# A state-space mixer whose norm adds up a group's squares one tile of weights later

## The chip, the core and the metric

The kernel runs as one program on one core of a Trainium2 chip. A core has engines with a queue of instructions each: TensorE (PE in the rows, with PEld for the loading of weights into it), VectorE (DVE), ScalarE (ACT), GpSimd (POOL) and SyncE (SP, which here issues transfers). They run side by side and wait for one another by semaphores. The time is the device time of one launch in microseconds. Three runs of the kernel before took 2009.55, 2011.78 and 2013.37 us; their median, 2011.78 us, is the time that is compared.

## What is computed

The reference is a block of a diffusion generator with two layers over 512 tokens of 1024 channels (256 context tokens, 256 latent tokens). Layer 0 mixes tokens by a state-space scan (SSD), layer 1 by retention, and each ends in a mixture of experts. The change lies in the SSD mixer, in the last step of `ssd_branch`:

```python
y = y_f + rev(y_b) + xs * d_skip.reshape(SSD_GROUPS, SSD_HPG)[..., None]
y = y.reshape(bsz, seqlen, SSD_D_INNER) * jax.nn.silu(proj[..., :SSD_D_INNER])
yg = y.reshape(bsz, seqlen, SSD_GROUPS, SSD_D_INNER // SSD_GROUPS).astype(jnp.float32)
yg = yg * lax.rsqrt(jnp.mean(jnp.square(yg), -1, keepdims=True) + LN_EPS)
return yg.reshape(bsz, seqlen, SSD_D_INNER).astype(dtype) * norm_w, h_f, h_b
```

The 2048 inner channels form four groups of 512. For each token and group the output of the scan is multiplied by a gate, and the result is divided by the root of the mean of its squares over the group. That root's reciprocal is called the factor here: 512 tokens by 4 groups, kept as a 128x4 tile for each group. It is used only when the output projection is evicted, since it can be multiplied in behind that product.

## The kernel before

The class `SSD` runs over a list `tiles` of weight tiles: `dt`, then for each group three `x` tiles (convolution inputs: one channel block each for the scan's B and C, and four for x) and two `z` tiles (the gate), then the output tiles `o`. A weight tile comes in by a transfer into a ring (`ringA`), ScalarE rounds it to a short form (`wh`, line 440) and GpSimd subtracts to get the remainder (`wl`, line 441). A block of 128 channels takes 24 products of 128x512 into the PSUM tile `pin`, eight steps of three products each: lines 719, 720 and 721. For an `x` block ScalarE copies `pin` to `pad` and starts `cacc`, VectorE adds the four other taps of the convolution (line 750), ScalarE takes a tanh (`cth`, line 752) and VectorE finishes `cacc` (line 759). TensorE transposes it (`ptr`, line 733) and ScalarE stores it as `xtok` (line 734). For a `z` block ScalarE takes a tanh (`zth`) and VectorE makes `sz` (line 777).

Beside these tiles runs work of the groups. The dictionary `side` says behind which tile each piece is called, and the table `PACE` gives the place as an offset from the last `x` tile of the group: the scan's start (`do_scan`), its four chunks (`do_chunk`), and the gate (`do_gate`). In the list the last `x` tile of group g is followed by `z` 0 and `z` 1 of g and then by `x` 0, 1 and 2 of group g+1, so offset 4 is the tile `x` 1 of group g+1 and offset 5 its `x` 2, behind which the scan of g+1 also starts. The calls fix what waits for what. The order in which the instructions then stand on each engine is drawn up by the framework's scheduler; scans and chunks are called at a raised priority. An engine takes its instructions strictly in that order.

The gate makes four rounds of transposes (line 1029) and products with `sz` (line 1031) into `yT`. Then ScalarE squares `yT` (line 1035), GpSimd adds the squares in two steps (lines 1036 and 1037), TensorE adds over partitions by four products with a column of ones (`pms`, line 1040), VectorE scales (`ms`, line 1042) and takes a reciprocal square root by small steps on 128x4 (`rsq`: lines 220 to 223, which each read one tile, and three rounds of 228, 229 and 230, which each read two), and copies the factor to `srs` (line 1045). For groups 0 to 2 `yT` is stored to memory by a transfer (`ytd`, line 1048).

The start of a scan makes `xs` on GpSimd (line 946, from `xtok`), the products `pcb` (line 961) and `ph` (line 948) on TensorE, and copies `ph` to the state `h` on VectorE (line 951). `ph` has one PSUM buffer (tag `y`), so the second `ph` waits for the copy of the first. `ptr`, `pms` and `pcb` share a tag of two buffers (`tp`). GpSimd also makes `sk` (line 1000).

Of the kernel before, what the change touches and what calls it, by code (L numbers as in the profile page):

```python
# [11 lines left out]
F32 = mybir.dt.float32  # L12
# [10 lines left out]
P = 128  # L23
# [113 lines left out]
class Ring:  # L137
# [3 lines left out]
    def __init__(self, nc):  # L141
        self.nc, self.src, self.at, self.tiles, self.pending = nc, [], {}, {}, []
        self.pools, self.finished, self.slot = {}, set(), {}
# [66 lines left out]
def col(S, name, a=0, b=None):  # L210
    o, w = CL[name]
    return S.c[:, o + a:o + (w if b is None else b)]


def rsqrt(S, v, n, eps, pool):

    V = S.nc.vector
    t = pool.tile([P, 4, n], F32, name="rsq", tag="rsq%d" % n, bufs=2)
    x, y, h, q = (t[:, j] for j in range(4))
    V.tensor_scalar(x, v, eps, None, op0=OP.add)  # L220
    V.tensor_scalar(q.bitcast(I32), x.bitcast(I32), 1, None, op0=OP.logical_shift_right)
    V.tensor_scalar(y.bitcast(I32), q.bitcast(I32), -1, 0x5F3759DF, op0=OP.mult, op1=OP.add)
    V.tensor_scalar(h, x, -0.5, None, op0=OP.mult)
    for _ in range(3):
        if n == 1:
            V.scalar_tensor_tensor(q, y, h, y, op0=OP.mult, op1=OP.mult)
        else:
            V.tensor_tensor(q, y, y, OP.mult)
            V.tensor_tensor(q, q, h, OP.mult)
        V.scalar_tensor_tensor(y, q, 1.5, y, op0=OP.add, op1=OP.mult)  # L230
    return y
# [328 lines left out]

SSD_MODS = [(0, 1), (0, 2), (1, 0)]

PACE = [(0, 1, 2, 3, 3, 4)] * 3 + [(0, 0, 1, 1, 1, 3)]


PRI = (0, 0)
# [4 lines left out]
class SSD:  # L571
    def __init__(self, S, A):
        self.S, self.A = S, A
        tiles = [("dt",)] + [("x", 0, q) for q in range(3)]
        for g in range(3):
            tiles += [("z", g, u) for u in range(2)] + [("x", g + 1, q) for q in range(3)]
        tiles += [("z", 3, u) for u in range(2)]
        for g in range(4):
            tiles += [("o", g, u) for u in range(2)]

        self.side = side = {t: [] for t in tiles}
        side["x", 0, 1].append(("steps",))
        for g in range(4):
            at = tiles.index(("x", g, 2))
            for it, n in zip([("scan", g)] + [("chunk", g, c) for c in range(4)] + [("gate", g)], PACE[g]):
                side[tiles[at + n]].append(it)
        side["z", 3, 1] += [("early", 0), ("ysplit", 0)]
        side["o", 2, 1].append(("early", 1))
        side["o", 0, 0] += [("close",), ("ysplit", 1)]
        side["o", 1, 0].append(("ysplit", 2))  # L590
        side["o", 2, 0].append(("ysplit", 3))
        mods = deque(("m", l, q, k) for l, q in SSD_MODS for k in range(8))
        for t in tiles[2:26]:
            if mods:
                side[t].append(mods.popleft())
        self.tiles = tiles
# [422 lines left out]
    def do_gate(self, g):  # L1019

        S = self.S
        nc, w1, w2 = S.nc, self.w1, self.w2
        V, AC, T_ = nc.vector, nc.scalar, nc.tensor
        y, sz = self.y, self.sz.pop(g)
        yT = self.yT[g] = self.yp.tile([P, 4, 512], F32, name="yT")
        for c in range(4):
            pt = self.psum([P, 4, 128], "ptr", "tp")
            for j in range(4):
                T_.transpose(pt[:, j, :], y[:, c, j * 128:(j + 1) * 128], col(S, "ident"))
            t = slice(c * 128, (c + 1) * 128)  # L1030
            V.tensor_tensor(yT[:, :, t], pt, sz[:, :, t], OP.mult)

        sq = [w2.tile([P, 2, 512], F32, name="sq", tag="ee") for _ in range(2)]
        for j in range(2):
            AC.activation(sq[j], yT[:, 2 * j:2 * j + 2], AF.Square)
        nc.gpsimd.tensor_tensor(sq[0], sq[0], sq[1], OP.add)
        nc.gpsimd.tensor_tensor(sq[0][:, 0], sq[0][:, 0], sq[0][:, 1], OP.add)
        pm = self.psum([P, 4], "pms", "tp")
        for i in range(4):
            T_.matmul(pm[:, i:i + 1], sq[0][:, 0, i * 128:(i + 1) * 128], S.ones[:, 0:1], start=True, stop=True)  # L1040
        ms = w2.tile([P, 4], F32, name="ms")
        V.tensor_scalar(ms, pm, 1.0 / 512, None, op0=OP.mult)
        rs = rsqrt(S, ms, 4, 16 * EPS, w2)
        self.rs[g] = S.const.tile([P, 4], F32, name="srs", tag="srs%d" % g)
        V.tensor_copy(self.rs[g], rs)
        if g < 3:
            S.ytd[g] = S.dram.tile([P, 2048], F32, name="ytd", tag="ytd%d" % g)
            nc.sync.dma_start(S.ytd[g], yT.rearrange("p a l -> p (a l)"))


    def norm_setup(self, pool):
# [27 lines left out]
    def build(self):  # L1079
        S, A = self.S, self.A  # L1080
        nc = S.nc
        V, AC, G = nc.vector, nc.scalar, nc.gpsimd
        with ExitStack() as es, ExitStack() as es2:
# [39 lines left out]
            bcast(S, A["ssd_d_skip"], self.dsk)  # L1123
            AC.activation(self.nega, self.dtc[:, 1:2], AF.Exp)
            V.tensor_scalar(self.nega, self.nega, -1.0, None, op0=OP.mult)
            self.Btok, self.BT, self.CT, self.sz, self.yT, self.yhl, self.rs = ({} for _ in range(7))
            S.ytd = {}
            tiles = self.tiles
            prep = lambda n: split_tile(S, tiles[n], self.wp)
# [1152 lines left out]
```

## Time and profile before

| What | Value |
|---|---|
| Median of three runs | 2011.78 us |
| The profiled execution | 2005.95 us |
| Its span | 2004.2 us |
| Mean granted TensorE clock | 0.954 of full |
| TensorE busy | 1769.8 us, 88% |
| VectorE busy | 953.0 us, 48% |
| ScalarE busy | 489.4 us, 24% |
| GpSimd busy | 456.8 us, 23% |

The span is the time between the first and the last instruction of the profiled execution; its own time has 1.75 us around it. Busy shares are means over stages with different limits: the SSD mixer lies between about 90 and 600 us of the span, the first mixture of experts follows it. A row of a timeline gives a start, a duration, an engine, a line, an operation with what it writes and reads, and a count; a bracket at its end is the idle time of that engine ahead of it and what ended it. A queue's order does not tell times, and a busy engine may be one that is held.

### The profile page before, as it was taken

What the parts mean: (1) busy time and instruction counts of PE and PEld (TensorE: products, weight loads), DVE (VectorE), ACT (ScalarE), POOL (GpSimd) and SP (SyncE); (2) the same over time, 40 slices, a digit from 0 to 9 for tenths busy, and PEclk for the clock granted to TensorE, in tenths of its full rate; (3) what the DMA queues carried; (4) which work ended last, traced back from release to release, by engine and by line L of the source; (5) the groups of instructions that cost most, each with busy time, mean ns of one, the idle gap of its engine ahead of it and who ended that gap; (6) DMA issues with size and microseconds to landing.
All of it is one profiled execution on the core that took longest, in us unless ns stands there. A gap on an engine that the chain in (4) does not pass through costs nothing. (4 is left out here: it accounts for less than half of the span.)

```text
span 2004.2 us, 23517 instructions
## 1 busy us (share of the span) xinstructions
PE 1769.8 (88%) x9021; PEld 1002.5 (50%) x9021; DVE 953.0 (48%) x1685; ACT 489.4 (24%) x827; POOL 456.8 (23%) x275
## 2 busy tenths in 40 slices
PE   6899999999986999998999789988897998788886
PEld 3665666666764433332332488776873432123221
DVE  3847575765696434433243566474454432103112
ACT  2555454543212100000000233232232100000000
POOL 2343425343345000000000243454551100000000
PEclk8999999999997999999999899999997999989998
DMA  7423323336735999999999744474367999999996
GB/s 284 150 99 116 126 95 136 111 111 220 275 109 223 371 399 399 373 383 401 409 406 368 290 149 146 155 263 145 113 255 294 409 409 409 409 375 407 409 409 242
DMA packets 138022, 543.84 MB, mean 271 GB/s; under 512 B 10320, under 2 KB 10832, under 8 KB 125360
## 3 DMA queue, kind: packets, MB, share of 16 engines
q1 hardware_dynamic: 137328, 541.80, 69.9%
q8 instruction: 73, 1.20, 0.2%
q10 hardware_dynamic: 576, 0.48, 0.1%
q14 instruction: 45, 0.37, 0.0%
HBM read 537.00 MB, written 5.24 MB: 271 GB/s over the span
## 5 line engine op out<-in xcount | busy, mean ns | idle before, releaser
L441 POOL TENSOR_TENSOR wl<-ringA,wh 128x1024 fp32r<-128x1024 f32 x116 | 290.0, 2512 | 812.0 <-ACT wh L440 794.0
L440 ACT ACTIVATE wh<-ringA 128x1024 fp32r<-128x1024 f32 x118 | 124.3, 1058 | 225.5 <-PE pin L720 61.0
L720 PE MATMUL pin<-u,wh 128*128 128x512 f32 x304 | 132.0, 434 | 0.0
L1868 PE MATMUL pd<-ringB,hT 128*32 128x512 f32 (+1 forms) x472 | 123.0, 617 | 6.0 <-ACT hT L1858 4.5
L721 PE MATMUL pin<-u,wl 128*128 128x512 f32 x304 | 127.4, 419 | 0.0
L719 PE MATMUL pin<-u,wh 128*128 128x512 f32 x304 | 126.9, 417 | 0.0
L1879 DVE SCALAR_TENSOR_TENSOR yh<-pd,ws,yh 128x512 fp32r<-128x512 f32 x40 | 30.0, 751 | 198.1 <-ACT yh L1878 196.2
L1839 PE MATMUL pg<-ringE,xT 128*32 128x512 f32 (+1 forms) x312 | 110.4, 609 | 7.7 <-DMA ringE<-in_moe_w_gate_up_dram 7.2
L1839 PE MATMUL pu<-ringE,xT 128*32 128x512 f32 (+1 forms) x312 | 110.6, 609 | 3.6 <-DMA ringE<-in_moe_w_gate_up_dram 3.6
L1844 ACT ACTIVATE th<-pg 128x512 f32<-128x512 f32 x22 | 13.1, 597 | 402.9 <-PE pg L1839 392.8
L1848 DVE SCALAR_TENSOR_TENSOR th<-th,pg 128x512 f32<-128x512 f32 x22 | 15.1, 687 | 200.0 <-ACT th L1844 200.0
L750 DVE SCALAR_TENSOR_TENSOR cacc<-pad,cw,cacc 128x512 f32<-128x512 f32 x96 | 94.3, 986 | 13.6 <-ACT cacc L748 12.7
L2143 POOL TENSOR_TENSOR oacc<-oacc,ringX 128x512 f32<-128x512 f32 x1 | 1.6, 1623 | 432.6 <-ACT oacc L207 432.6
L1201 PE MATMUL pin<-u,wh 128*128 128x256 f32 (+1 forms) x256 | 84.9, 332 | 16.1 <-DVE gT L1253 10.0
L1911 DVE TENSOR_TENSOR tl<-pc,ringB 128x512 f32<-128x512 f32 x124 | 81.1, 685 | 37.1 <-PE pc L1886 35.3
L1839 PE MATMUL pg<-ringB,xT 128*32 128x512 f32 (+1 forms) x268 | 89.2, 613 | 5.9 <-DMA ringB<-in_moe_w_gate_up_dram 5.9
L1839 PE MATMUL pg<-ringA,xT 128*32 128x512 f32 (+1 forms) x244 | 85.7, 617 | 6.7 <-DMA ringA<-in_moe_w_gate_up_dram 6.2
L1778 PEld LDWEIGHTS px<-oh,hhl 128*128 128x128 f32 x576 | 73.3, 193 | 34.7 <-issue 32.2
L1839 PE MATMUL pu<-ringB,xT 128*32 128x512 f32 (+1 forms) x268 | 89.6, 609 | 0.9 <-DMA ringB<-in_moe_w_gate_up_dram 0.8
L1886 PE MATMUL pc<-yh,os 128*128 128x512 f32 x248 | 82.6, 432 | 8.0 <-DVE tl L1911 7.4
L1868 PE MATMUL pd<-ringE,hT 128*32 128x512 f32 (+1 forms) x240 | 77.1, 601 | 10.0 <-DMA ringE<-in_moe_w_down_dram 7.2
L1839 PE MATMUL pu<-ringA,xT 128*32 128x512 f32 (+1 forms) x244 | 83.1, 615 | 1.8 <-DMA ringA<-in_moe_w_gate_up_dram 1.8
(414 smaller groups left out, 3907.5 us busy)
## 6 DMA issues: line engine op xcount, KB each, us to landing
ringE<-in_moe_w_gate_up_dram SPq DMA_DIRECT2D x76, 1024.0 KB, 18.1
ringB<-in_moe_w_gate_up_dram SPq DMA_DIRECT2D x63, 1024.0 KB, 17.3
ringA<-in_moe_w_gate_up_dram SPq DMA_DIRECT2D x55, 1024.0 KB, 17.6
ringB<-in_moe_w_down_dram SPq DMA_DIRECT2D x53, 1024.0 KB, 18.0
ringA<-in_mod_w_dram SPq DMA_DIRECT2D x40, 1024.0 KB, 4.9
ringF<-in_moe_w_gate_up_dram SPq DMA_DIRECT2D x34, 1024.0 KB, 17.7
ringX<-in_moe_w_gate_up_dram SPq DMA_DIRECT2D x28, 1024.0 KB, 18.1
ringE<-in_moe_w_down_dram SPq DMA_DIRECT2D x28, 1024.0 KB, 18.2
```

What stands on the lines that cost most here:

```text
L440: S.split = nc.scalar.activation(hi, w, AF.Copy).ins
L441: (eng or nc.gpsimd).tensor_tensor(lo, w, hi.bitcast(F32), OP.subtract)
L719: S.nc.tensor.matmul(p, h, self.uh(k), start=k == 0, stop=False)
L720: S.nc.tensor.matmul(p, h, self.ul(k), start=False, stop=False)
L721: S.nc.tensor.matmul(p, l, self.uh(k), start=False, stop=k == 7)
L750: nc.vector.scalar_tensor_tensor(acc, pad[:, :, t:t + 256], cw[:, m, t:t + 1], acc, op0=OP.mult, op1=OP.add)
L1201: self.S.nc.tensor.matmul(p, a, self.uh(k)[:, T], start=k == 0, stop=False)
L1778: nc.tensor.matmul(px[:, b, :], self.S.hhl[i][:, m, j * 128:(j + 1) * 128], oh[:, i], start=i == 0 and m == 0, stop=i == nt - 1 and m == 1)
L1839: nc.tensor.matmul(po[o:o + n, :], xT[:, k, a:a + n], w.get(k)[:, u * 512:(u + 1) * 512], start=k == 0, stop=k == 7)
L1868: nc.tensor.matmul(pd[u % n][o:o + m, :], hT[:, j, a:a + m], w.get(8 + j)[:, u * 512:(u + 1) * 512], start=j == 0, stop=j == 3)
L1886: self.S.nc.tensor.matmul(pc, os_[s, i * 128:(i + 1) * 128], ys[q][s, u % n], start=q == 0, stop=q == 1)
L1911: V.tensor_tensor(t, pc, self.gate(i)[:, c], OP.mult)
```

## The change

The part of the gate behind the two additions on GpSimd becomes a function of its own, `do_factor`. `PACE` gets a seventh entry for it: 5 for groups 0 to 2, which is one tile behind the gate, and 3 for group 3, the same tile as the gate. The tile with the added squares is kept in a dictionary between the two calls, and the store of `yT` is called right behind the additions. No instruction is added or removed.

```diff
-PACE = [(0, 1, 2, 3, 3, 4)] * 3 + [(0, 0, 1, 1, 1, 3)]
+PACE = [(0, 1, 2, 3, 3, 4, 5)] * 3 + [(0, 0, 1, 1, 1, 3, 3)]
...
-            for it, n in zip([("scan", g)] + [("chunk", g, c) for c in range(4)] + [("gate", g)], PACE[g]):
+            for it, n in zip([("scan", g)] + [("chunk", g, c) for c in range(4)] + [("gate", g), ("factor", g)], PACE[g]):
...
         nc.gpsimd.tensor_tensor(sq[0], sq[0], sq[1], OP.add)
         nc.gpsimd.tensor_tensor(sq[0][:, 0], sq[0][:, 0], sq[0][:, 1], OP.add)
+        self.sq[g] = sq[0]
+        if g < 3:
+            S.ytd[g] = S.dram.tile([P, 2048], F32, name="ytd", tag="ytd%d" % g)
+            nc.sync.dma_start(S.ytd[g], yT.rearrange("p a l -> p (a l)"))
+
+    def do_factor(self, g):
+
+        S, w2, sq = self.S, self.w2, self.sq.pop(g)
+        V, T_ = S.nc.vector, S.nc.tensor
         pm = self.psum([P, 4], "pms", "tp")
         for i in range(4):
-            T_.matmul(pm[:, i:i + 1], sq[0][:, 0, i * 128:(i + 1) * 128], S.ones[:, 0:1], start=True, stop=True)
+            T_.matmul(pm[:, i:i + 1], sq[:, 0, i * 128:(i + 1) * 128], S.ones[:, 0:1], start=True, stop=True)
         ms = w2.tile([P, 4], F32, name="ms")
         V.tensor_scalar(ms, pm, 1.0 / 512, None, op0=OP.mult)
         rs = rsqrt(S, ms, 4, 16 * EPS, w2)
         self.rs[g] = S.const.tile([P, 4], F32, name="srs", tag="srs%d" % g)
         V.tensor_copy(self.rs[g], rs)
-        if g < 3:
-            S.ytd[g] = S.dram.tile([P, 2048], F32, name="ytd", tag="ytd%d" % g)
-            nc.sync.dma_start(S.ytd[g], yT.rearrange("p a l -> p (a l)"))
```

What stands where then? First TensorE's queue behind the gate of group 0, as the difference between before (-) and now (+); `ptr` here is the transpose of an `x` block of group 1, and the changed kernel's line 1048 is line 1040 of before.

```order
 L719 MATMUL pin<-u,wh 128x512
 L720 MATMUL pin<-u,wh 128x512
-L721 MATMUL pin<-u,wl 128x512
-L719 MATMUL pin<-u,wh 128x512
-L1040 MATMUL pms<-ones,sq 128x1 x4
-L720 MATMUL pin<-u,wh 128x512
-L721 MATMUL pin<-u,wl 128x512
-L719 MATMUL pin<-u,wh 128x512
-L720 MATMUL pin<-u,wh 128x512
 L733 MATMUL ptr<-c,cacc 128x128 x4
```

The first `ptr` now stands six products, and the squares' four, earlier than before. The second `ptr`, which has kept its place among the products, stands 20 of them behind the first, where it was 14.

Next the same queue some rows later, at the start of the scan of group 1; the `L720` of the second row is the fourth product behind the second `ptr`.

```order
 L719 MATMUL pin<-u,wh 128x512
 L720 MATMUL pin<-u,wh 128x512
+L1048 MATMUL pms<-ones,sq 128x1 x4
+L721 MATMUL pin<-u,wl 128x512
+L719 MATMUL pin<-u,wh 128x512
 L961 MATMUL pcb<-CT,BT 128x128 x4
 L948 MATMUL ph<-xs,Btok 128x512
```

The squares' products now stand ahead of `pcb`, with two products between; four products and the second `ph` follow `ph` in both kernels.

Then VectorE's queue at that place, before: the small steps end ahead of `sz` (line 777), and the copy of the first state `h` (line 951) comes right behind it.

```order
L228 TENSOR_TENSOR rsq<-rsq 128x4
L759 SCALAR_TENSOR_TENSOR cacc<-cth,cacc 128x512
L229 TENSOR_TENSOR rsq<-rsq 128x4
L230 SCALAR_TENSOR_TENSOR rsq<-rsq 128x4
L228 TENSOR_TENSOR rsq<-rsq 128x4
L229 TENSOR_TENSOR rsq<-rsq 128x4
L230 SCALAR_TENSOR_TENSOR rsq<-rsq 128x4
L1045 COPY srs<-rsq 128x4
L777 SCALAR_TENSOR_TENSOR sz<-zth,pin 128x512
L951 COPY h_1571<-ph 128x512
```

And now:

```order
L777 SCALAR_TENSOR_TENSOR sz<-zth,pin 128x512
L220 TENSOR_SCALAR rsq<-ms 128x4
L221 TENSOR_SCALAR rsq<-rsq 128x4
L223 TENSOR_SCALAR rsq<-rsq 128x4
L222 TENSOR_SCALAR rsq<-rsq 128x4
L228 TENSOR_TENSOR rsq<-rsq 128x4
L229 TENSOR_TENSOR rsq<-rsq 128x4
L230 SCALAR_TENSOR_TENSOR rsq<-rsq 128x4
L228 TENSOR_TENSOR rsq<-rsq 128x4
L229 TENSOR_TENSOR rsq<-rsq 128x4
L230 SCALAR_TENSOR_TENSOR rsq<-rsq 128x4
L951 COPY h_1571<-ph 128x512
```

Ten of the small steps have come to stand between `sz` and the copy of `h`; ahead of line 759 there are none now. In group 1 all thirteen and the copy to `srs` stand ahead of the copy of `h`, in group 2 six of them and an addition of the scan's (`ee`, line 987). GpSimd's queue has the same order as before in groups 0 and 1: two `xs`, `sk`, and then a `wl` and two `xs` in group 0, the two `xs` and then a `wl` in group 1; in group 2 the `wl` has moved ahead of the third `xs`. The rest of the queues of these groups is the same but for neighbours that change places, save that in group 2 the first `ptr` stands among products of a modulation, ahead of where `pms` was.

## Rows read from the trace of the kernel before

**Rows 1.** Busy time by stretch of 100 us (stretch, its length, busy us and count of PE, PEld, DVE, ACT and POOL, granted clock, DMA share, GB/s): a stretch of the SSD stage, and one of the expert stage behind it.

```profile
200.00:300.00 100.00, 94.21 (x452) 64.89 (x452) 66.79 (x97) 46.31 (x84) 37.79 (x33) 1.00 0.30 110
...
700.00:800.00 100.00, 93.60 (x559) 37.30 (x552) 39.40 (x75) 7.71 (x15) 0.00 (x0) 1.00 1.02 404
```

**Rows 2.** Whom TensorE waited for between 180 and 520 us (total us, times, longest us).

```profile
PE pms L1040 <- POOL sq L1037: 9.7, 4, 3.3
```

**Rows 3.** Timeline around the squares' products of group 0; columns: start in us, duration in us, engine, line, operation, tiles and shapes, count, and in brackets the idle time ahead with what ended it.

```profile
197.04 2.46 DVE L759 SCALAR_TENSOR_TENSOR cacc<-cth,cacc 128x512 f32<-128x512 f32 x1 [1.14 <-ACT cth L752]
...
197.73 0.39 PE L720 MATMUL pin<-u,wh 128*128 128x512 f32 x1
...
199.42 1.75 DVE L750 SCALAR_TENSOR_TENSOR cacc<-pad,cw,cacc 128x512 f32<-128x512 f32 x1
200.58 2.83 POOL L441 TENSOR_TENSOR wl<-ringA,wh 128x1024 fp32r<-128x1024 f32 x1
...
200.67 1.05 PE L1040 MATMUL pms<-ones,sq 128*128 128x1 f32 x8 [2.08 <-POOL sq L1037]
...
201.84 2.12 DVE L750 SCALAR_TENSOR_TENSOR cacc<-pad,cw,cacc 128x512 f32<-128x512 f32 x1
...
204.80 0.74 DVE L750 SCALAR_TENSOR_TENSOR cacc<-pad,cw,cacc 128x512 f32<-128x512 f32 x1
...
205.58 0.63 ACT L752 ACTIVATE cth<-cacc 128x512 f32<-128x512 f32 x1 [1.76 <-DVE cacc L750]
...
206.33 0.68 DVE L759 SCALAR_TENSOR_TENSOR cacc<-cth,cacc 128x512 f32<-128x512 f32 x1
...
207.07 0.66 PE L733 MATMUL ptr<-c,cacc 128*128 128x128 f32 x4 [0.68 <-DVE cacc L759]
```

**Rows 4.** The same timeline, a little later: the start of the scan of group 1.

```profile
207.48 0.48 PE L720 MATMUL pin<-u,wh 128*128 128x512 f32 x1
...
207.80 0.39 PE L721 MATMUL pin<-u,wl 128*128 128x512 f32 x1
...
208.03 0.40 PE L719 MATMUL pin<-u,wh 128*128 128x512 f32 x1
...
208.44 2.04 POOL L946 TENSOR_TENSOR xs<-xtok,tokv 128x512 f32<-128x512 f32 x2 [2.69 <-ACT xtok L734]
208.49 1.08 PE L961 MATMUL pcb<-CT,BT 128*128 128x128 f32 x8
...
209.54 1.12 PE L948 MATMUL ph<-xs,Btok 128*128 128x512 f32 x2
...
210.70 0.69 DVE L951 COPY h<-ph 128x512 f32<-128x512 f32 x1 [1.09 <-PE ph L948]
...
211.51 0.30 PEld L948 LDWEIGHTS ph<-xs,Btok 128*128 128x128 f32 x2 [0.36 <-POOL sk L1000]
```

**Rows 5.** Timeline, the same place of group 1.

```profile
301.15 2.47 DVE L759 SCALAR_TENSOR_TENSOR cacc<-cth,cacc 128x512 f32<-128x512 f32 x1 [1.93 <-ACT cth L752]
...
304.80 1.05 PE L1040 MATMUL pms<-ones,sq 128*128 128x1 f32 x8 [2.09 <-POOL sq L1037]
...
305.97 2.09 DVE L750 SCALAR_TENSOR_TENSOR cacc<-pad,cw,cacc 128x512 f32<-128x512 f32 x1
...
313.36 2.22 DVE L1045 COPY srs<-rsq 128x4 f32<-128x4 f32 x1
...
315.52 2.04 POOL L946 TENSOR_TENSOR xs<-xtok,tokv 128x512 f32<-128x512 f32 x2
...
316.61 1.12 PE L948 MATMUL ph<-xs,Btok 128*128 128x512 f32 x2 [1.82 <-POOL xs L946]
```

**Rows 6.** Timeline, the same place of group 2.

```profile
403.48 0.68 DVE L759 SCALAR_TENSOR_TENSOR cacc<-cth,cacc 128x512 f32<-128x512 f32 x1
...
407.22 0.40 PE L719 MATMUL pin<-u,wh 128*128 128x512 f32 x1
...
409.71 2.35 POOL L441 TENSOR_TENSOR wl<-ringA,wh 128x1024 fp32r<-128x1024 f32 x1
...
409.80 1.05 PE L1040 MATMUL pms<-ones,sq 128*128 128x1 f32 x8 [2.18 <-POOL sq L1037]
```

**Rows 7.** Small steps of a reciprocal square root elsewhere (the norm behind the mixer), in the timelines of POOL (first row) and of DVE (the next two).

```profile
582.23 2.83 POOL L207 TENSOR_TENSOR tok<-oacc,sca 128x1024 f32<-128x1024 f32 x1
...
582.74 0.20 DVE L207 TENSOR_SCALAR rsq<-rsq 128x1 int32<-128x1 int32 x2
582.98 2.10 DVE L207 SCALAR_TENSOR_TENSOR rsq<-rsq 128x1 f32<-128x1 f32 x1
```

**Rows 8.** All instructions on the tiles rsq, one row of them: duration in ns, least, median and most.

```profile
L229 DVE TENSOR_TENSOR rsq<-rsq x12: 155/161/165, 205.9 to 495.6; 128x4 f32<-128x4 f32 x12
```

**Rows 9.** Busy time by stretch of 10 us, columns as in the first group.

```profile
200.00:210.00 10.00, 8.65 (x47) 6.92 (x48) 7.86 (x21) 3.47 (x6) 5.10 (x6) 1.00 0.48 174
300.00:310.00 10.00, 7.91 (x37) 6.03 (x32) 8.18 (x12) 4.12 (x7) 6.90 (x5) 0.83 0.65 220
...
410.00:420.00 10.00, 10.00 (x50) 7.80 (x50) 7.32 (x27) 5.27 (x12) 3.43 (x3) 0.83 0.38 140
490.00:500.00 10.00, 9.52 (x32) 7.95 (x33) 6.47 (x22) 1.75 (x2) 0.61 (x2) 0.66 0.88 325
```

**Rows 10.** The transfers of expert weights into the ring E among the instructions on that tile: issue time in ns, first and last start in us.

```profile
L186 SPq DMA_DIRECT2D ringE<-in_moe_w_gate_up_dram x76: 368/1790/5597, 468.4 to 1944.1; - x76
```

More of the change, by code (lines that the diff above doesn't have):

```diff
@@ L1125, in build @@
             V.tensor_scalar(self.nega, self.nega, -1.0, None, op0=OP.mult)
-            self.Btok, self.BT, self.CT, self.sz, self.yT, self.yhl, self.rs = ({} for _ in range(7))
+            self.Btok, self.BT, self.CT, self.sz, self.yT, self.yhl, self.rs, self.sq = ({} for _ in range(8))
             S.ytd = {}
```

## The prediction

> **What bounds the kernel now.** I read the stretches first, then the waits, then the timelines of the three places. In the SSD stage TensorE is busy 94.21 of 100 us and the transfers 0.30 of it; in the expert stage behind it the transfers are busy throughout, 1.02 [rows 1]. So in the SSD stage time is lost where TensorE stands still. The expert weights do not start early enough to take such a loss back: the first of their transfers is issued at 468.4 us, behind all three places that the change touches [rows 10]. I count a microsecond of TensorE's idle time there as one of the end.
>
> Of those idle times the longest sum in 180 to 520 us is that of the squares' products, which wait for GpSimd's second addition: 9.7 us in four [rows 2]. Three belong to groups 0 to 2: 2.08, 2.09 and 2.18 us [rows 3, 5, 6]. The fourth is group 3's, which the change leaves where it was. Near them are smaller ones: in group 0 one of 0.68 us for the second transpose [rows 3] and one of 0.36 for the second state product `ph` [rows 4], in group 1 one of 1.82 for the first `ph` [rows 5]. That makes 3.12, 3.91 and 2.18 us at the three places.
>
> **What sets VectorE's pace.** The reader should see one thing in [rows 3]: line 759 has an ordinary length of 0.68 us (206.33), but the one at 197.04 took 2.46, and the next two instructions took 1.75 and 2.12 instead of 0.74. Each ended some 0.55 us behind an instruction of GpSimd: for the third this is visible, GpSimd's `wl` ending at 203.41 and VectorE's line 750 at 203.96. So while GpSimd works, VectorE's instructions with two tiles from SBUF get through one for each of GpSimd's. Group 1 shows the same lengths, 2.47 and 2.09 [rows 5]. It also holds the tiny ones: a step of the reciprocal root took 2.10 us beside GpSimd's 2.83 [rows 7], the copy of the 128x4 factor 2.22 [rows 5]; free, such a step takes 0.16 [rows 8] (0.2 with its handover). Steps that read one tile passed, two in 0.20 [rows 7], and so does the copy of `h`, which reads PSUM, 0.69 [rows 4].
>
> A page speaks against that last reading in part. By the Trainium skill, "SBUF — State Buffer", section "Who interferes with whom", steps that multiply by a constant can enter a mode that takes the shared pair of ports too, and would then be held like the others. The row of 0.20 us shows that they weren't; by the page the copy of `h` in group 0 would come some 0.7 us later, an estimate, and the sum would be up to 2 us higher over three groups.
>
> **The change, part by part.** Nothing is added or removed, so the cost is in waits alone. The store of `yT` is called earlier but waited for no small step before; SyncE has nothing behind it that TensorE awaits here: 0.
>
> *The wait for the squares goes.* The additions end at 200.67, and the products that read them now stand behind the second transpose, about 208: saved 2.08, 2.09 and 2.18 us.
>
> *The first transpose waits in its place.* It stands two products before the old place of the squares. TensorE got there at 200.67 - 2.08 = 198.59, less two products of 0.23 (the spacing at 207.80 and 208.03 [rows 4]) = 198.13. It reads line 759's result, which is held until 199.50, and 0.06 us of handover (207.01 to 207.07 in [rows 3]): idle 1.43. Group 1 the same: 301.15 + 2.47 + 0.06 = 303.68, against 304.80 - 2.09 - 0.46 = 302.25: 1.43. In group 2 line 759 ended at 404.16, ahead of the additions [rows 6]: 0.
>
> *The second transpose.* TensorE does four transposes (0.41, from 207.07 to 207.48) and 20 products, the first taking 0.32 to the next, the others 0.23 [rows 4], and a last one of 0.39 to its end: it is there at 199.56 + 0.41 + 0.32 + 18 x 0.23 + 0.39 = 204.82. VectorE's chain is still held until 203.96, as now; then two taps of 0.74, the tanh of 0.63, line 759 of 0.68 [rows 3] and 0.12 of handovers end at 206.87. Idle 2.05. Group 1: VectorE 305.97 + 2.09 + 2.91 = 310.97 [rows 5], TensorE 303.68 + 5.26 = 308.94: 2.05. Group 2: the third tap is held by `wl` until 409.71 + 2.35 + 0.55 = 412.61, then comes an addition of the scan (0.68), one tap, the tanh and line 759: 415.4. TensorE passes the old place at 407.62 (the product of 407.22 ended then [rows 6]) and has 19 products of 0.23 to do, counting four of the decay's like the others: 412.0. Idle 3.4.
>
> *The second `ph`.* Here the small steps stand ahead of the copy of `h`, and GpSimd is at work. Group 0: the squares' products start at 206.87 + 0.41 + 1.01 = 208.3 and take about 0.9, two products 0.55, so `pcb` starts at 209.75. From `pcb` to the place of the second `ph` it was 211.51 - 0.36 - 208.49 = 2.66 us [rows 4]: TensorE arrives at 212.4. VectorE has `ms` at 209.4, `sz`, four steps that pass, and then six that don't. GpSimd starts `xs` 1.37 us behind the transpose (207.07 to 208.44 [rows 3, 4]), so 208.24; the pair takes 2.04, `sk` as much as one of them, 1.02, `wl` 2.35 when itself not delayed [rows 6], the third `xs` 1.02. The first three held steps go out at 211.3, 213.65 and 214.65. The fourth `xs` waits for the second `ph`, so GpSimd rests, and three steps of 0.2 and the copy of 0.69 end at 216.0: idle 3.6. Group 1: `pcb` at 310.97 + 0.41 + 1.01 + 0.9 + 0.55 = 313.8, first `ph` reached at 314.9, but its `xs` still stands behind a `wl` and starts at 315.52 [rows 5]: ready at 316.55, idle 1.65. The second `ph` is reached 1.6 later, at 318.2; nine steps and the copy to `srs` stand ahead of `h`. `wl`, two `xs`, `sk` and the third `xs` let five through by 319.65, the other five take 1.0, the copy 0.69: 321.35, idle 3.15. Group 2: `pms` at 417.1, `pcb` at 418.6, second `ph` reached at 421.2; the addition `ee` and two steps go out behind `sk` (419.9), `wl` (422.3) and the third `xs` (423.3), the copy ends at 424.0: idle 2.8.
>
> *Sum of the idle times.* Group 0: 1.43 + 2.05 + 3.6 = 7.1 against 3.12, +4.0. Group 1: 1.43 + 2.05 + 1.65 + 3.15 = 8.3 against 3.91, +4.4. Group 2: 0 + 3.4 + 2.8 = 6.2 against 2.18, +4.0. Together +12.4.
>
> *The clock.* Behind the gaps of groups 1 and 2 a stretch of 10 us shows a granted clock of 0.83, a part of it at 1.2 instead of 2.4 GHz: 1.7 us lost in each. Behind group 0's gap of 2.08 it stayed at 1.00, behind group 3's of 3.33 it is 0.66: 3.4 lost [rows 9]. So gaps of 2.1 us sometimes bring a fall and one of 3.3 did. Now four gaps are of 2.8 us and more, and I count 1.7 us for each, less the two falls that go: +3.4. The bounds: no more falls than now, 0; or 3.4 for each of the four and 1.7 for the two of 2.05, less 3.4: +13.6.
>
> Total +15.8. The profiled execution of before, 2005.95 us with a span of 2004.2, would become 2021.75; it lies 5.8 below the median of the runs, 2011.78, and to that I add: **2027.6 us**.
>
> **Rivals.** *The wait changes its place and no more.* The first two transposes wait as above, but the small steps slip through beside GpSimd. For it: the steps that read one tile passed [rows 7], and the twelve of one kind (line 229) never took more than 0.165 [rows 8]. Against it: 2.10 and 2.22 us [rows 5, 7]. Then the idle times are 1.43 + 2.05 + 0.4 = 3.9, 1.43 + 2.05 + 1.65 = 5.1 and 3.4: +0.8, +1.2 and +1.2, one fall of the clock fewer, -1.7: +1.5, **2013.3**, with one fall more or less 2011.6 to 2015. That the change does nothing that can be measured would read the same.
>
> *Faster: VectorE's chain arrives first.* If line 759 and the taps were issued ahead of GpSimd's additions, each at its free length, the first `cacc` would be done 1.8 us sooner (0.68 in place of 2.46), the second some 2.4 (0.74 for 1.75 and 2.12), and both transposes would find it. Then idle time of 0.4 and 1.65 is left in groups 0 and 1: -2.7, -2.3, in group 2 -2.2, and the clock gives back 3.4: **2001.2**. It decides where line 759 ends before 198.1. Against it: the change leaves what stands ahead of line 759, and GpSimd's first addition, as they were, and the row that shows 2.46 is of them [rows 3].
>
> **Chances.** The forecast 0.63, the first rival 0.22, the faster one 0.12, others 0.03. A difference under 0.2% (4 us) can't be told from none in a measurement of this kernel. The forecast is slower by more than that even at 2018, where half the idle time and no clock is lost; its own range is 2018 to 2037. The whole range reaches down to the first rival and leaves out the faster one: 2008 to 2036. Faster 0.14, same 0.23, slower 0.63.
>
> **What would show it.** Right: no wait of TensorE for GpSimd's additions in groups 0 to 2, but waits of 1.4 and 2.05 us for `cacc` and of 2.8 to 3.6 for the copy of `h`; steps of the reciprocal root of 1 to 2.4 us ahead of that copy; lower granted clock at 210, 320 and 420 us. Wrong: small steps of 0.16 us beside `sk` and `wl` (the first rival), or line 759 of group 0 at 0.7 us (the second).

## The result and the profile after

Six runs of the changed kernel gave 2018.79 to 2024.35 us with a median of 2022.82; six of the kernel before, in the same comparison, a median of 2010.66. The ratio is 1.0061 with a 95% interval of 1.0042 to 1.0081. That is 12 us slower, where 15.8 had been forecast, and 2022.82 us where 2027.6 had.

The issue of the expert weights into the ring E in the changed kernel, as in [rows 10]:

```profile
L186 SPq DMA_DIRECT2D ringE<-in_moe_w_gate_up_dram x76: 367/1856/5721, 486.1 to 1960.6; - x76
```

The profiled execution's span grew by 16.8 us (2021.0 against 2004.2), and the first transfer of expert weights is issued at 486.1 us instead of 468.4. So the loss is complete before the expert stage starts, and nothing of it comes back later but the last 0.9 us.

Whom TensorE waited for between 180 and 540 us, in total, how often, and the longest:

```profile
PE ptr L733 <- DVE cacc L759: 14.0, 8, 2.2
PE ph L948 <- DVE rsq L230: 3.6, 1, 3.6
PE pms L1048 <- POOL sq L1036: 3.3, 1, 3.3
PE ph L948 <- DVE rsq L228: 3.0, 1, 3.0
PE ph L948 <- DVE h L951: 3.0, 1, 3.0
```

The transposes' row before was:

```profile
PE ptr L733 <- DVE cacc L759: 5.6, 4, 1.8
```

The squares' products waited 9.7 us in four times [rows 2]; what is left is the one wait of group 3. In its place the transposes `ptr` wait 14.0 us in eight times, where it was 5.6 in four, and three waits of the second `ph`, of 3.0 to 3.6 us, are new. Two of these are put down to a small step `rsq`: that is VectorE's queue, in which the copy of `h` had its turn late.

Now group 0, where [rows 3 and 4] were, as a timeline (start, duration, engine, line, operation, tiles, and the idle time ahead in brackets):

```profile
197.39 2.45 DVE L759 SCALAR_TENSOR_TENSOR cacc<-cth,cacc 128x512 f32<-128x512 f32 x1 [1.15 <-ACT cth L752]
...
199.99 0.63 PE L733 MATMUL ptr<-c,cacc 128*128 128x128 f32 x4 [1.51 <-DVE cacc L759]
...
207.35 1.12 PE L733 MATMUL ptr<-c,cacc 128*128 128x128 f32 x4 [2.17 <-DVE cacc L759]
...
212.18 2.37 POOL L441 TENSOR_TENSOR wl<-ringA,wh 128x1024 fp32r<-128x1024 f32 x1
212.28 2.30 DVE L221 TENSOR_SCALAR rsq<-rsq 128x4 int32<-128x4 int32 x1
...
214.49 0.16 DVE L223 TENSOR_SCALAR rsq<-rsq 128x4 f32<-128x4 f32 x1
214.50 1.05 POOL L946 TENSOR_TENSOR xs<-xtok,tokv 128x512 f32<-128x512 f32 x1
214.61 0.97 DVE L222 TENSOR_SCALAR rsq<-rsq 128x4 int32<-128x4 int32 x1
215.61 0.16 DVE L228 TENSOR_TENSOR rsq<-rsq 128x4 f32<-128x4 f32 x1
...
216.68 0.68 DVE L951 COPY h<-ph 128x512 f32<-128x512 f32 x1
...
217.51 2.05 PE L948 MATMUL ph<-xs,Btok 128*128 128x512 f32 x2 [3.02 <-DVE rsq L228]
```

Read it from the end. The second `ph` (217.51) waited 3.02 us for the buffer that the copy of `h` (216.68) sets free. That copy stood behind the small steps, and they behind GpSimd: line 221 took 2.30 us, until GpSimd's `wl` was done, line 222 took 0.97, until `xs` was done, and the steps with two tiles, from 215.61 on, took 0.16 each, since GpSimd had no work left. Further up are the two waits for `cacc`: 1.51 us behind a line 759 of 2.45, and 2.17.

The second `ph` of groups 1 and 2, and the waits ahead of it there:

```profile
310.84 0.63 PE L733 MATMUL ptr<-c,cacc 128*128 128x128 f32 x4 [1.48 <-DVE cacc L759]
...
318.20 0.66 PE L733 MATMUL ptr<-c,cacc 128*128 128x128 f32 x4 [2.16 <-DVE cacc L759]
...
327.65 2.05 PE L948 MATMUL ph<-xs,Btok 128*128 128x512 f32 x2 [3.00 <-DVE h L951]
```

```profile
426.86 0.66 PE L733 MATMUL ptr<-c,cacc 128*128 128x128 f32 x4 [1.76 <-DVE cacc L759]
...
436.47 2.05 PE L948 MATMUL ph<-xs,Btok 128*128 128x512 f32 x2 [3.57 <-DVE rsq L230]
```

And the clock, in those stretches of 10 us between 190 and 470 in which it was below 1.00 (columns as in [rows 1]; the clock is the third value from the end):

```profile
200.00:210.00 10.00, 7.83 (x33) 6.30 (x34) 6.49 (x5) 2.41 (x5) 4.74 (x5) 0.86 0.49 184
210.00:220.00 10.00, 6.98 (x29) 4.77 (x28) 7.39 (x19) 1.56 (x3) 5.92 (x6) 0.84 0.01 2
220.00:230.00 10.00, 9.66 (x49) 6.29 (x49) 4.51 (x8) 3.23 (x5) 3.07 (x2) 0.96 0.36 120
320.00:330.00 10.00, 6.91 (x30) 4.46 (x29) 7.21 (x18) 0.60 (x1) 5.53 (x6) 0.83 0.01 2
330.00:340.00 10.00, 10.00 (x46) 6.36 (x44) 3.40 (x5) 3.03 (x5) 3.21 (x2) 0.82 0.44 157
430.00:440.00 10.00, 6.43 (x26) 4.43 (x25) 9.09 (x17) 3.02 (x6) 6.29 (x5) 0.80 0.00 0
440.00:450.00 10.00, 10.00 (x30) 6.64 (x29) 5.08 (x11) 0.06 (x1) 2.08 (x2) 0.69 0.00 0
```

I count the clock lost as (1 - clock) x 10 us for a stretch: 1.4 + 1.6 + 0.4 in group 0, 1.7 + 1.8 in group 1, 2.0 + 3.1 in group 2, 12.0 in all. Before it was 1.7 each in groups 1 and 2, 3.4 [rows 9]. The idle time of the three places is 1.51 + 2.17 + 3.02 = 6.70, 1.48 + 2.16 + 3.00 = 6.64 and 1.76 + 3.57 = 5.33, together 18.67, against 9.21 by the prediction's count. Before there was one more wait in group 2, of 0.98 us for `xs`, which has gone. So 8.5 us of idle time and 8.6 of clock make 17.1, and the stage grew by 17.4 in this execution: from the last waiting transposes of group 0's gate (193.06 and 193.41) to the first transfer of expert weights it was 275.3 us and is 292.7.

The two stages as one stretch each, before and now (columns as in [rows 1]), give the same split without counting gaps:

```profile
193.06:468.40 275.34, 256.18 (x1201) 173.83 (x1202) 189.58 (x274) 129.55 (x230) 111.63 (x85) 0.99 0.31 112
```

```profile
193.41:486.10 292.69, 263.93 (x1201) 178.47 (x1202) 198.51 (x274) 129.71 (x230) 109.24 (x85) 0.96 0.29 105
```

The same 1201 instructions keep TensorE busy for 7.75 us longer, and it stands still for 28.76 us in place of 19.16, 9.60 more: together the 17.35 us by which the stage grew. The count by stretches gives 8.6 for the clock because it takes in the parts of a stretch in which TensorE stands still; the 9.60 hold, beside the 8.5, small waits such as 0.7 us more of the products `py` (line 992).

### The profile page after: what moved, and what is told of

Read it like the earlier page. It is cut to its first block, busy times and chain, and to the rows that moved or that the text cites. A ratio compares the mean times of both kernels' runs of the same rounds, so it can differ in the third digit from the quotient of the medians.

```text
span 2021.0 us, 23520 instructions
## 1 busy us (share of the span) xinstructions
PE 1778.2 (88%) x9021; PEld 1009.4 (50%) x9021; DVE 965.2 (48%) x1685; ACT 489.9 (24%) x827; POOL 452.6 (22%) x275
## 5 line engine op out<-in xcount | busy, mean ns | idle before, releaser
L720 PE MATMUL pin<-u,wh 128*128 128x512 f32 x304 | 134.7, 443 | 0.0
L750 DVE SCALAR_TENSOR_TENSOR cacc<-pad,cw,cacc 128x512 f32<-128x512 f32 x96 | 97.1, 1015 | 13.6 <-ACT cacc L748 12.4
L1206 PE MATMUL pin<-u,wh 128*128 128x256 f32 (+1 forms) x256 | 84.7, 332 | 12.4 <-DVE gT L1258 9.7
## 6 DMA issues: line engine op xcount, KB each, us to landing
ringB<-in_moe_w_gate_up_dram SPq DMA_DIRECT2D x63, 1024.0 KB, 17.1
ringA<-in_moe_w_gate_up_dram SPq DMA_DIRECT2D x55, 1024.0 KB, 17.7
```

The lines of the kernel that those rows point to most:

```text
L720: S.nc.tensor.matmul(p, h, self.ul(k), start=False, stop=False)
L750: nc.vector.scalar_tensor_tensor(acc, pad[:, :, t:t + 256], cw[:, m, t:t + 1], acc, op0=OP.mult, op1=OP.add)
L1206: self.S.nc.tensor.matmul(p, a, self.uh(k)[:, T], start=k == 0, stop=False)
```

## Experiments

The theory after the result: two things cost. VectorE is held beside GpSimd, first by the additions (so the transposes wait for `cacc` in place of the squares' products) and then by `xs`, `sk` and `wl` (so the small steps hold up the copy of `h`); and each longer gap of TensorE is followed by a lower clock. The rivals: the early transposes alone cost it all; the place of the steps in the queue costs, whether GpSimd works or not; the earlier store has a part.

All times below are medians with ratios to the kernel before from the same comparison; a ratio can differ by 0.001 from the quotient of the two medians. Where it tells more, the stage of one trace is given as above (275.3 us before, 292.7 after), with the clock lost between 190 and 470 us.

**The small steps behind the copies of `h`.** `S.V` is VectorE with the order of the calls kept.

```diff
+    V = S.V if n == 4 else S.nc.vector
...
+PACE = [(0, 1, 2, 3, 3, 4, 5, 6)] * 3 + [(0, 0, 1, 1, 1, 3, 3, 3)]
...
-                V.tensor_copy(n, p)
+                S.V.tensor_copy(n, p)
...
-        rs = rsqrt(S, ms, 4, 16 * EPS, w2)
+        self.sq[g] = ms
+
+    def do_root(self, g):
+        S = self.S
+        rs = rsqrt(S, self.sq.pop(g), 4, 16 * EPS, self.w2)
```

> The changed kernel with the small steps and the copy to srs ordered behind the two copies of h in groups 0 to 2; TensorE's order is that of the changed kernel. Theory (the steps ahead of the copy of h, held beside GpSimd, cost 3.0 to 3.6 us a group, and the clock behind these gaps as much as 1.7 us each): the waits of the second ph (3.02, 3.00 and 3.57 us) go, those of the transposes for cacc (1.5 and 2.2 us) stay, the time falls by 9.6 us and some 4 of clock to about 2009 us, ratio to the kernel before 0.998 to 1.002. Rival (the loss comes from the early transposes and their clock, the copy of h is late for another reason, such as the later squares' products): the waits of ph stay near 3 us and the time near 2022 us, ratio 1.005 to 1.007.

Measured: 2010.89 us, ratio 1.0016 (0.9999 to 1.0033). Its waits:

```profile
PE ptr L733 <- DVE cacc L759: 14.0, 8, 2.2
PE py L992 <- DVE W L989: 4.3, 5, 1.3
```

The waits of `ph` are gone, those for `cacc` are the same 14.0 us to the tenth. The products `py` wait 4.3 us for the tiles `W`, which VectorE makes and ahead of which the steps now stand; it was 1.0 in the changed kernel. The stage took 278.0 us with 1.7 of clock lost: 14.7 less than the changed kernel. As one stretch:

```profile
193.63:471.60 277.97, 255.52 (x1201) 172.85 (x1202) 194.14 (x274) 129.80 (x230) 110.92 (x85) 0.99 0.31 111
```

TensorE stands still for 22.45 us, 6.3 less (9.6 less of one wait, 3.3 more of another), and is busy for 8.4 less, which makes the 14.7. The clock counted by stretches is 10.3 less; the 1.9 between lie in gaps and would be counted twice. So the steps' place ahead of the copy of `h` carries 14.7 of the 17.4 us of the traces, the clock behind it included, and by the ratios 0.0045 of the 0.0061. The first rival falls.

**The changed kernel without the small steps.**

```diff
-        rs = rsqrt(S, ms, 4, 16 * EPS, w2)
+        rs = ms
```

> The changed kernel without the small steps of the reciprocal root in all four groups: the mean of the squares is copied as the factor, so its output is scaled otherwise and later routing may differ a little. Theory: as the kernel with late steps, waits of ph under 0.5 us, about 2008 us, ratio 0.997 to 1.001; if this is more than 3 us below the kernel with late steps, the steps cost something at their later place too. Rival: near 2022 us.

Measured: 2010.33 us, ratio 1.0017 (1.0003 to 1.0031), a little above what was expected; no wait of `ph` for VectorE, stage 276.1 us with 3.4 of clock lost. TensorE is busy for 256.93 us of the stage and stands still for 19.18, as before (19.16). So the early transposes' waits cost no more than the waits which they replaced, and the idle time that the change added is that of the small steps. Against the kernel with late steps TensorE stands still for 3.3 us less (`py` waits 1.9 us in place of 4.3), so the steps cost something at their later place too; the stage is only 1.9 us shorter, since more clock was lost. The median doesn't show it: in this trace what follows the first expert transfer takes 1542.0 us (2011.4 - 469.4) where it takes 1535.8 before, and another factor means another routing, so its total is no measure of the steps.

**Only group 0's factor late.**

```diff
+PACE = [(0, 1, 2, 3, 3, 4, 5)] + [(0, 1, 2, 3, 3, 4, 4)] * 2 + [(0, 0, 1, 1, 1, 3, 3)]
```

> Only group 0's factor one tile later, groups 1 and 2 as before. Theory (each group adds its own idle time and clock): group 0's 3.6 us of idle time more and about 3 of lost clock, 6 to 7 us in the trace between 200 and 240 us, nothing in groups 1 and 2: about 2016 us, ratio 1.002 to 1.004. Rival (the loss is one thing of the whole stage, as the earlier store of yT or a later start of the expert weights): the whole of the loss or none of it, ratio 1.006 or 1.000.

Measured: 2013.01 us, ratio 1.0019 (1.0005 to 1.0032), a third of the changed kernel's loss and the lower end of what was expected. The trace shows group 0's waits of the changed kernel and groups 1 and 2's of before:

```profile
201.06 0.63 PE L733 MATMUL ptr<-c,cacc 128*128 128x128 f32 x4 [1.50 <-DVE cacc L759]
...
208.43 1.09 PE L733 MATMUL ptr<-c,cacc 128*128 128x128 f32 x4 [2.17 <-DVE cacc L759]
...
218.63 1.95 PE L948 MATMUL ph<-xs,Btok 128*128 128x512 f32 x2 [2.99 <-DVE rsq L228]
```

```profile
313.05 1.05 PE L1048 MATMUL pms<-ones,sq 128*128 128x1 f32 x8 [2.05 <-POOL sq L1036]
```

Its stage is 6.9 us longer than before: TensorE stands still for 23.01 us, 3.85 more, and is busy for 259.20, 3.0 more. That is what the theory gave for one group by itself; groups 1 and 2 alone were not tried.

**Without GpSimd's additions.**

```diff
-        nc.gpsimd.tensor_tensor(sq[0], sq[0], sq[1], OP.add)
-        nc.gpsimd.tensor_tensor(sq[0][:, 0], sq[0][:, 0], sq[0][:, 1], OP.add)
```

> The changed kernel without GpSimd's two additions of squares in all four groups (only a fourth of the squares is summed, so the factor is too large). Theory (these additions hold VectorE's line 759 and taps): line 759 of group 0 takes 0.7 instead of 2.45 us, the first transposes' waits of 1.5 us go, the second ones' of 2.2 shrink to under 1, group 3's wait of 3.3 goes, the waits of ph of about 3 us stay: 2022.8 less about 11 and some 4 of clock, 2006 to 2011 us, ratio 0.998 to 1.000. Rival (VectorE is held by something else, the wl or its own queue): waits for cacc stay at 1.5 and 2.2 us, only group 3's 3.3 and its clock go, 2016 us.

Measured: 2021.33 us, ratio 1.0068 (1.0046 to 1.009): neither what the theory said of the time nor what the rival said. Of the waits it was right in one half:

```profile
198.17 0.69 DVE L759 SCALAR_TENSOR_TENSOR cacc<-cth,cacc 128x512 f32<-128x512 f32 x1 [1.14 <-ACT cth L752]
...
199.10 0.60 PE L733 MATMUL ptr<-c,cacc 128*128 128x128 f32 x4
...
199.39 5.14 DVE L750 SCALAR_TENSOR_TENSOR cacc<-pad,cw,cacc 128x512 f32<-128x512 f32 x4 [0.53 <-ACT cacc L748]
...
200.32 2.87 POOL L441 TENSOR_TENSOR wl<-ringA,wh 128x1024 fp32r<-128x1024 f32 x1 [3.01 <-ACT wh L440]
...
205.97 0.66 PE L733 MATMUL ptr<-c,cacc 128*128 128x128 f32 x4 [1.70 <-DVE cacc L759]
...
215.45 2.04 PE L948 MATMUL ph<-xs,Btok 128*128 128x512 f32 x2 [3.84 <-DVE rsq L228]
```

Line 759 takes 0.69 us and the first transposes don't wait: the additions were what held it. But `wl`, which no longer stands behind them, now starts at 200.32, 1.4 us earlier counted from the start of the stage, while VectorE's four taps run, and holds them: 5.14 us for four, which took 6.14 in the changed kernel. The second transposes wait 1.70 here and 2.03 in group 1, and the second `ph` 3.84, 3.01 and 3.63. The stage is 286.0 us, 6.7 less than the changed kernel's, and the wait of group 3 is gone too; the trace's span is 5.1 less. But the trace is that of the fastest of six runs (2017.68 us). Their median is 1.5 us under the changed kernel's, and the ratio, 1.0068, is not under its 1.0061. So it is shown that the additions hold line 759, and not that leaving them out saves time. What takes the stage's 6.7 us back wasn't settled; the output of this kernel differs, and so may its routing.

**The small steps on PSUM tiles, at their place ahead of `h`.** The tiles that hold the mean, x, the shifted value and y lie in PSUM, `h` (here -x/2, not the scan's state) and `q` in SBUF, so a step reads one tile from SBUF at most.

```diff
+        V = self.S.V
+        pr = self.psum([P, 16], "prs", "py")
+        ms, x, i, y = (pr[:, 4 * j:4 * j + 4] for j in range(4))
...
+        for _ in range(3):
+            V.tensor_tensor(q, y, h, OP.mult)
+            V.tensor_tensor(q, y, q, OP.mult)
+            V.scalar_tensor_tensor(y, q, 1.5, y, op0=OP.add, op1=OP.mult)
```

> The changed kernel with the small steps at the same place, ahead of the copy of h, but on tiles in PSUM, so that no step reads two tiles from SBUF or both reads and writes SBUF alone; the third round's algebra is the same, y(yh) for (yy)h. Theory (the steps cost because GpSimd's work holds VectorE's use of SBUF): each step takes 0.16 to 0.25 us beside GpSimd, thirteen take 2.6 us, the waits of ph in groups 0 and 1 fall from 3.0 to under 0.7 us; about 2011 to 2014 us, ratio 1.000 to 1.003 (in group 2 two products W have come ahead of h, so its wait may stay). Rival (their number and place in the queue is what costs, or the lower clock): waits of ph in groups 0 and 1 stay above 2 us, ratio 1.005 to 1.007.

Measured: 2013.97 us, ratio 1.0036 (1.0024 to 1.0049). The timeline of group 0 (line 207 is the helper behind `S.V`, the tiles `prs` lie in PSUM):

```profile
211.96 0.57 DVE L207 TENSOR_SCALAR prs<-prs 128x4 f32<-128x4 f32 x3
212.07 2.38 POOL L441 TENSOR_TENSOR wl<-ringA,wh 128x1024 fp32r<-128x1024 f32 x1
...
212.57 0.16 DVE L207 TENSOR_SCALAR rsq<-prs 128x4 f32<-128x4 f32 x1
...
212.77 0.36 DVE L207 TENSOR_TENSOR rsq<-prs,rsq 128x4 f32<-128x4 f32 x2
...
214.62 0.68 DVE L207 COPY h<-ph 128x512 f32<-128x512 f32 x1
...
216.18 1.02 PE L948 MATMUL ph<-xs,Btok 128*128 128x512 f32 x2
```

All thirteen steps and the copy to `srs` stand ahead of the copy of `h` here, where ten steps stood, beside the same `wl`, and none is held: three of one kind in 0.57 us, two in 0.36, one in 0.16. The copy of `h` starts at 214.62 and the second `ph` doesn't wait, nor in group 1. The second rival falls: it is not the steps' number or place alone, but where their tiles lie while GpSimd works. The time is above what the theory gave by a little. In group 2 two products `W` had come to stand among the steps, and there `py` waited 2.1 us for `srs`; the transposes' 14.0 us are still in it. The stage took 281.8 us.

**Only the store earlier.**

```diff
+PACE = [(0, 1, 2, 3, 3, 4, 4)] * 3 + [(0, 0, 1, 1, 1, 3, 3)]
```

> The changed code with the factor at the gate's own tile, so that alone the call of the store of yT is earlier than in the kernel before. Theory: no effect, ratio 0.999 to 1.001, waits as before (2.1, 2.1, 2.2, 3.3 us for the squares). Rival (the store's place on SyncE's queue, or the new function's order, has a part in the loss): ratio above 1.002.

Measured: 2007.09 us, ratio 0.9996 (0.9986 to 1.0006). The waits for the squares are 2.09, 2.09, 2.18 and 3.33 us, as before. No part of the store can be seen. The clock lost in its stage was 5.1 us though, where before it was 3.4 with the same waits for the squares: the same gaps don't always bring the same fall.

**The additions on VectorE, in the kernel before.** This and the next three look for a version that beats both.

```diff
-        nc.gpsimd.tensor_tensor(sq[0], sq[0], sq[1], OP.add)
-        nc.gpsimd.tensor_tensor(sq[0][:, 0], sq[0][:, 0], sq[0][:, 1], OP.add)
+        V.tensor_tensor(sq[0], sq[0], sq[1], OP.add)
+        V.tensor_tensor(sq[0][:, 0], sq[0][:, 0], sq[0][:, 1], OP.add)
```

> The kernel before with the two additions of squares on VectorE instead of GpSimd; the scheduler then draws the squares' products four products later. Theory (VectorE loses its time by being held beside GpSimd, not by its own work): line 759 and the taps behind the additions take 0.7 us but for those beside wl, the four waits for the squares (2.1, 2.1, 2.2, 3.3 us) fall to under 0.7 each, and the clock does not fall behind them: 9 us and up to 6 of clock, ratio 0.993 to 0.997. Rival (the additions cost VectorE as much as it was held, 1.8 us, so the waits move to the transposes): ratio 0.999 to 1.002.

Measured: 2005.91 us, ratio 0.9982 (0.9971 to 0.9994). Faster than before, by less than was expected.

```profile
198.23 1.23 DVE L1036 TENSOR_TENSOR sq<-sq 128x1024 f32<-128x1024 f32 x1 [0.63 <-ACT sq L1035]
...
199.38 0.69 DVE L759 SCALAR_TENSOR_TENSOR cacc<-cth,cacc 128x512 f32<-128x512 f32 x1
...
199.98 0.68 DVE L1037 TENSOR_TENSOR sq<-sq 128x512 f32<-128x512 f32 x1
...
207.23 0.66 PE L733 MATMUL ptr<-c,cacc 128*128 128x128 f32 x4 [1.00 <-DVE cacc L759]
...
207.39 2.38 POOL L441 TENSOR_TENSOR wl<-ringA,wh 128x1024 fp32r<-128x1024 f32 x1 [1.43 <-ACT wh L440]
207.48 2.31 DVE L228 TENSOR_TENSOR rsq<-rsq 128x4 f32<-128x4 f32 x1
```

The additions cost VectorE 1.23 and 0.68 us and line 759 is free; the squares' products don't wait in groups 0 to 2, and 1.84 us in group 3. But the next `wl`, which now goes ahead of `xs`, starts at 207.39 and meets the last small steps, one of which takes 2.31 us. So `xs` comes behind that `wl` and the copy of `h` behind the held steps: the `ph` wait 0.89 and 1.26 us in group 0, 1.57 and 0.67 in group 1.

**Both: the additions on VectorE and the small steps late.** The edits of the first and the last kernel together.

> The changed kernel with the small steps behind the copies of h, and with the two additions on VectorE. Theory: as the kernel with late steps (ratio 1.0016), less the first transposes' waits of 1.5 us each in part and group 3's wait of 3.3 with its clock: 0.995 to 0.999. With the squares' products late nothing waits for them, so it would be equal to or better than additions on VectorE in the old order. Rival: wl, freed of the additions ahead of it, starts earlier and holds the taps instead, so the second transposes' waits stay at 2 us: 0.999 to 1.001, all gain from group 3.

Measured: 2007.32 us, ratio 0.9997 (0.9987 to 1.0006), stage 273.4 us. The second transposes wait 1.84 and 1.81 us behind taps that `wl` holds, and `py` 4.3 us for `W`. That is the rival's mechanism and its time.

**The additions on VectorE and the small steps on PSUM tiles, at the gate's tile.** The edits shown for each, with 4 as the seventh entry of `PACE`, without `S.V`.

> The kernel before with the additions on VectorE and the small steps on PSUM tiles, at the gate's tile. Theory (what was left in the kernel with additions on VectorE, the waits of the second ph for h of 1.26 and 0.67 us in groups 0 and 1, are small steps held beside a wl that now starts earlier): these waits go, those for xs (0.89, 1.57) and for cacc (1.0) stay; about 2 us less than additions on VectorE alone, ratio 0.996 to 0.998. Rival (the steps are no longer on the path there): 0.998 to 0.999, equal to additions on VectorE alone.

Measured: 2002.62 us, ratio 0.9971 (0.9956 to 0.9987): the lowest ratio of all, 6 us under the kernel before and, by the two ratios, 18 under the changed one. Its waits:

```profile
PE ptr L733 <- DVE cacc L759: 6.2, 5, 1.8
...
PE ph L948 <- POOL xs L946: 4.3, 3, 1.6
```

No `ph` waits for VectorE any more, but the waits for `xs`, which were expected to stay, grew from 2.5 us in two to 4.3 in three. The second transposes wait 0.64 and 0.62 us, and in none of the 10-us stretches between 190 and 470 us is the clock below 1.00. The stage takes 268.8 us. The step in time against additions on VectorE alone is 2 us in the ratios' middle, as expected, but the intervals overlap, so the runs don't show it; the stages of the two traces are 268.8 and 274.0 us.

**The same with ordinary small steps behind the copies of `h`.** The seventh entry of `PACE` is 4, the eighth 6.

> The kernel before with the additions on VectorE, the squares' products at the gate's tile and the small steps behind the copies of h. Theory: the waits for h of 1.26 and 0.67 us go as with steps on PSUM, but the products W of the first chunk are held behind steps beside GpSimd, about 1 us a group as in the kernel with late steps: ratio 0.997 to 0.999. Rival: the squares' products in their early place bring back waits for cacc of 1.5 us and more, 0.999 to 1.001.

Measured: 2008.39 us, ratio 0.9996 (0.9982 to 1.0011). The waits for `cacc` in groups 0 and 1 are 0.90 and 0.85 us, so the rival's reason is not seen, but `py` waits 3.4 us for `W`, and the time is the rival's: by the ratios' middle late steps give back what the additions gain, though the intervals overlap.

**The changed kernel once more.** No edit.

> The changed kernel once more, for a second trace and a narrower interval. Theory (idle time of 18.7 us in the three places against 9.2, and clock falls behind most of these gaps): stage up to the first transfer of expert weights 14 to 18 us longer than before, ratio 1.006 to 1.009. Rival (the first trace is an outlier and the loss is the 12 us of the first medians, with little clock in it): stage 10 to 13 us longer, ratio 1.005 to 1.006.

Measured: 2022.69 us, ratio 1.0063 (1.0047 to 1.0079). The waits for `cacc` are 14.0 us again, the three of `ph` are 1.4, 2.1 and 3.6, the clock lost 12.0, the stage 290.1 us, 14.8 more than before; both figures lie in the theory's ranges. So the first trace was no outlier in its kind, only at the upper end: by the two ratios the loss is 12 to 13 us, by the medians 12 and 15. The trace of before was at the lower end, 2005.95 against a median of 2010.66.

## Why the prediction was right

It said slower, by 15.8 us, for two kinds of wait and the clock; it is slower by 12, and the trace shows these waits. The mechanism was right; that the sum came so near is in part luck, since two of its terms were off in opposite directions. By its steps:

- *The wait for the squares goes*: right in groups 0 to 2, shown by the waits after.
- *The first transpose waits in its place*: 1.43, 1.43 and 0 forecast, 1.51, 1.48 and 0 measured. That the additions hold line 759 was shown by leaving them out (0.69 us in place of 2.45).
- *The second transpose*: 2.05 twice forecast, 2.17 and 2.16 measured; in group 2 3.4 forecast and 1.76 measured. There VectorE's chain was right (2.8 us from the end of the held tap to the end of line 759, measured 2.7, from 424.14 to 426.80). TensorE's way was counted too short by 2.1 us, nearly all of it ahead of the old place of the squares: two sets of four transposes that now stand there were left out, 0.41 and 0.59 us, and the second cuts the modulation's eight products (line 321) in two, two in 1.05 us and six in 1.06, where the eight took 1.06.
- *The second `ph`*: 3.6, 3.15 and 2.8 forecast, 3.02, 3.00 and 3.57 measured. The sizes hold but for group 2's, the steps that make them are other ones. The prediction had four steps pass and the ones with two tiles wait; in fact lines 221 and 222, which read one tile, were held in group 0 for 2.30 and 0.97 us, and the ones with two tiles found GpSimd at rest; in group 1 two of each kind were held, for 0.96 to 0.97 us each. The reading that failed is "Steps that read one tile passed": it rested on steps of 128x1 [rows 7], and these are 128x4. The sentence that was set against it, from the Trainium skill, "SBUF — State Buffer", section "Who interferes with whom", by which `tensor_scalar` can take the shared pair, agrees with 2.30 us. The same section's rule that an instruction of VectorE with at most one SBUF input and outside these modes does not contend agrees with the 0.16 us of the steps on PSUM tiles.
- *The first `ph` of group 1*: an idle time of 1.65 for `xs` was forecast and none came. I had left the `wl` ahead of `xs` at its time of before. It moved with the rest: `xs` now starts 3.06 us behind the second transposes (321.26 - 318.20), where the prediction's numbers had 4.55 (315.52 - 310.97).
- *Sum of the idle times*: +12.4 forecast, 18.67 - 9.21 = +9.5 measured, or +8.5 with the 0.98 that went; TensorE's idle time of the whole stage grew by 9.6.
- *The clock*: +3.4 forecast, +8.6 measured by stretches and +7.75 as TensorE's busy time, inside the bounds of 0 to 13.6. This is the term that was mis-sized. It counted one fall of 1.7 us for each long gap; the falls were of 3.4, 3.5 and 5.1 us in the three places. The idle time was forecast too high and the clock too low by more; the two errors stand against each other, so that 15.8 came out nearer to the traces' 16.8 than either term to its own.
- *A microsecond there is one of the end*: right, 17.7 us at the first expert transfer and 16.8 at the end of the trace.

The first rival had the small steps slip through beside GpSimd, and they didn't (line 221 took 2.30 us). For the rest of the change it is near: with the steps out of the way of `h` the ratio is 1.0016, without them 1.0017, and in the latter the stage's idle time is that of before. The faster rival needed line 759 done before the additions start, and it took 2.45 us as before.

## What to carry to other kernels

A wait that is moved back is worth only what stands at its new place: look up which engine works beside it there, and what the moved instructions stand ahead of in their own queue. Six to thirteen steps on a 128x4 tile, 0.16 us each when free, cost 3.0 to 3.6 us a group here because a copy that TensorE waits for stood behind them while GpSimd worked; the same steps with operands in PSUM cost none of it in the two groups where they stood alone. And where a slow engine's work holds another's, moving that work to the one that was held can be cheaper than a new order; here it was cheaper than every order tried: 1.9 us of additions on VectorE in place of 4 on GpSimd, with the steps in PSUM, gave 0.9971.

## What the runs showed that was not expected

Lines 221 and 222, which read one 128x4 tile and write one, were held beside GpSimd for up to 2.32 us (line 222 of group 2), while two steps of the same operation on 128x1 went through in 0.20 beside an addition of 2.83 [rows 7]. Line 223 between them took 0.16: it started as one GpSimd instruction ended and the next began (214.49, 214.50). Which property of the operand decides was not tried.

The clock fell differently behind the same gaps. Group 0's wait of 2.08 us brought no fall in the trace of before [rows 9], and behind 2.09 us in the kernel with the store alone earlier the stretch of 200 to 210 us shows 0.66, 3.4 us lost. Two traces of the changed kernel both lost 12.0 us in the stage though their waits of `ph` were 9.6 and 7.1 us in sum. The best kernel, whose longest gap in the stage is 1.84 us, lost nothing there; the one with additions on VectorE alone, with the same longest gap, lost 3.4 us. How far the clock falls could not be told from a gap's length.
